# A two-layer encoder on one core: GpSimd negates weight halves between its two DMAs, and two query and key tiles change PSUM banks

## The chip, the core and the metric

The kernel runs on one core of a Trainium2 chip. The metric is device time in microseconds (us) of one execution, lower is better. The engines are TensorE (PE in the rows; PEld is its weight load), VectorE (DVE), ScalarE (ACT), GpSimd (POOL) and SyncE (SP). Each engine works through its own instructions strictly in their order, and waits at an instruction until what it needs is there. DMAs are issued by an engine's queue and land later.

## The reference, cut to what matters

Two layers; each mixes 512 tokens of 1024 channels by attention heads and a recurrent branch side by side, and then goes through a gated MLP. All of it is float32.

```python
def reference(x, g_mix, w_in, ...):
    for l in range(DEPTH):                       # DEPTH = 2
        h = rmsnorm(x, g_mix[l])
        z = h @ w_in[l]                          # 512 x 1024 by 1024 x 2560
        q, k, v, x_rec, gate = jnp.split(z, ...)  # 512 columns each
        att = neighbourhood_attention(q, k, v, rel_bias[l])
        xc = depthwise_conv(x_rec, conv_lru_w[l], conv_lru_b[l], LRU_PAD)
        rec = (rg_lru(xc, ..., reverse=False) + rg_lru(xc, ..., reverse=True)) * gelu(gate)
        mixed = concatenate([rmsnorm(att, g_att[l]), rmsnorm(rec, g_rec[l])])
        x = x + mixed @ w_out[l]
        h = rmsnorm(x, g_ffn[l])
        u_act, u_lin = jnp.split(h @ w_up[l], 2, axis=-1)
        u_act = depthwise_conv(u_act, conv_ffn_w[l], conv_ffn_b[l], (1, 1))
        x = x + (gelu(u_act) * u_lin) @ w_down[l]
    return rmsnorm(x, g_final)
```

## The kernel before

**Products in halves.** Each float32 operand is kept as two numbers: a leading half (`hi`, rounded to the format that TensorE reads) and the rest (`lo` = value - `hi`). One 128 x 128 block of weights times 512 tokens is three matmuls (`mm3`, L248 to L250): hi by hi, hi by the tokens' lo, lo by hi. So a product of a chunk of weights can start when its `hi` is there, but its third matmul (L250) needs `lo`.

**Weights.** `weight_plan` cuts all weights into chunks of eight blocks (128 x 1024 numbers, 512 KB; those of the recurrent gates have four blocks, 256 KB) in the order in which TensorE uses them. `chunk` hands out the next one and has `split_to` and `load_to` start the work on later ones. Most chunks come by SP's DMA as `raw` and are split by ScalarE and VectorE (L210, L211). Twenty chunks of the first layer, those of query, key, value, gate and the recurrent gates, are split without VectorE: GpSimd's queue issues a DMA that writes `hi` (L175), ScalarE writes `lo` = -`hi` (L200), and GpSimd's queue issues a second DMA that adds the same weights onto `lo` (L201). In the second layer these chunks come ready split, by SP. There are four buffers for `hi` and four for `lo`.

**The first layer's mixing stage.** Before it, four banks gather the recurrent input (tile `xr`) and the row sums of squares give the tokens' scale `g_mix_rb` (rows L387 to L401; GpSimd takes the power in between, L392). Then the list `MIX` gives the steps, in TensorE's order: `q`, `k`, `v`, `g` are the projections of one tile of 128 columns each (24 matmuls, an a and a b half), `t` the recurrent gates, `c` the convolution, `S` the scores of a head, `T` the transposes of its probabilities, `P` its product with the values, `u` the values turned to tokens. It runs four rounds, one for each pair of heads and each quarter of the recurrent channels; here they are called rounds one to four.

**What ScalarE and VectorE do there.** ScalarE evaluates the gates (L548 to L554), a square root for both directions (L560), the exponentials of the scores (L682) and the gelu (L636), and copies transposed tiles out of PSUM (L611 `vh`, L708 `pt`). VectorE finishes the gates (L555, L556, L562), runs two scans (L565, L568), reads the scores (L675), scales the probabilities (L684, L686), and writes the rests (`vl`, `pt`, L612 and L709). For the product `P`, GpSimd copies pieces of `vh` and `vl` into the tiles `edge` (L616).

**Order.** The program is recorded by a scheduler that places urgent work (`urgent`, and the negation with level 1) ahead of other work on each engine by its own estimate of times. The order on each engine is then fixed.

**Banks.** PSUM has eight banks of 128 x 512 numbers in four pools: `ps_mm` (three), `ps_s` (two, for the scores), `ps_pt` (two, for the transposes), `ps_o` (one).

Of the kernel before, what the change touches and what calls it, by code (L numbers as in the profile page):

```python
# [11 lines left out]
AF = mybir.ActivationFunctionType  # L12
ALU = mybir.AluOpType
# [87 lines left out]
def encoder(ctx: ExitStack, tc: tile.TileContext, x_d, w_d, cols_d, bias_d, out_d):  # L101
    nc = tc.nc
    plan = weight_plan()

    def pool(name, bufs, space=None):
        kw = {"space": space} if space is not None else {}
        return ctx.enter_context(tc.tile_pool(name=name, bufs=bufs, **kw))
# [16 lines left out]
    ps_mm = pool("ps_mm", 3, PS)  # L124
    ps_s = pool("ps_s", 2, PS)
# [3 lines left out]
    def big(pl, tag, name, dt=F32):  # L129
        return pl.tile([P, T], dt, tag=tag, name=name)  # L130

    def psum(pl, name):
        return pl.tile([P, T], F32, tag="ps", name=name)
# [6 lines left out]
    def f32(ap):  # L140
        return ap.bitcast(F32)

    def urgent(level=2):
        return tc.high_priority(offset=level * URGENT) if level else ExitStack()
# [6 lines left out]
    def pieces(i):  # L151
        return (slice(0, 1024),) if i else (slice(0, 512), slice(512, 1024))

    def width(i):
        return P * len(plan[i][2])

    def by_dma(i):

        w, _, bs = plan[i]
        return w == "gate" or w == "w_in" and bs[0][1] != 12  # L160

    def load_to(n):
        while state["load"] < min(n, len(plan)):
            i = state["load"]
            if by_dma(i):
                if i > state["use"] + 3:
                    return
                highs[i] = p_hi.tile([P, 1024], F32R, tag="hi", name=f"hi{i}")
                if i in kept:
                    lows[i] = p_lo.tile([P, 1024], F32R, tag="lo", name=f"lo{i}")  # L170
                    for n, t in enumerate((highs[i], lows[i])):
                        for h in range(width(i) // 512):
                            nc.sync.dma_start(f32(t[:, 512 * h:512 * h + 512]), kept[i][n, h])
                else:
                    nc.gpsimd.dma_start(highs[i][:, :width(i)], w_d[i][:, :width(i)])  # L175
                state["load"] += 1
                continue
            raws[i] = p_raw.tile([P, 1024], F32, tag="raw", name=f"raw{i}")
            for n, sl in enumerate(pieces(i)):
                nc.sync.dma_start(raws[i][:, sl], w_d[i][:, sl])  # L180
                if i == n == 0:
                    nc.sync.dma_start(x[0], x_d[0])
            state["load"] += 1

    def split_to(n):
        while state["split"] < min(n, len(plan)):
            i = state["split"]
            if by_dma(i) and i > state["use"] + 2:
                return
            load_to(i + 1)  # L190
            if i in kept:
                halves[i] = highs.pop(i), lows.pop(i)
                state["split"] += 1
                continue
            if i in highs:
                hi = highs.pop(i)
                lo = p_lo.tile([P, 1024], F32R, tag="lo", name=f"lo{i}")
                with urgent(1):
                    ws = slice(0, width(i))
                    nc.scalar.activation(lo[:, ws], f32(hi[:, ws]), AF.Copy, scale=-1.0)  # L200
                    nc.gpsimd.dma_start(lo[:, ws], w_d[i][:, ws], accum_op=ALU.add)  # L201
                halves[i] = (hi, lo)
                state["split"] += 1
                continue
            raw = raws.pop(i)
            hi = p_hi.tile([P, 1024], F32R, tag="hi", name=f"hi{i}")
            lo = p_lo.tile([P, 1024], F32R, tag="lo", name=f"lo{i}")
            with urgent(0):
                for sl in pieces(i):
                    nc.scalar.activation(hi[:, sl], raw[:, sl], AF.Copy)  # L210
                    nc.vector.tensor_tensor(out=lo[:, sl], in0=raw[:, sl], in1=f32(hi[:, sl]), op=ALU.subtract)  # L211
            halves[i] = (hi, lo)
            state["split"] += 1
# [22 lines left out]
    def chunk(w, l, first):  # L236
        i = state["use"]
        assert plan[i][0] == w and plan[i][1] == l and plan[i][2][0] == first, (plan[i], w, l, first)
        split_to(i + 1 + AHEAD_SPLIT)
        load_to(i + 1 + AHEAD_LOAD)  # L240
        state["use"] += 1
        return halves.pop(i)
# [26 lines left out]
    def column_parts(ps, w, l, m, rhs, step):  # L269
        c = chunk(w, l, (0, m))  # L270
        for k in range(8):
            mm3(ps, blk(c, k), rhs[k], k == 0, k == 7)
            if k % step == step - 1:
                yield
# [130 lines left out]
    def by_group(ap):  # L405
        return ap.rearrange("p (r g c) -> p g r c", r=ROWS, c=8)

    def in_group(ap):
        return ap.rearrange("p g (r c) -> p g r c", r=ROWS)
# [82 lines left out]
    def layer(l, xn):  # L492
# [79 lines left out]
        qk = {}  # L572

        def query_tile(i):
            ps = psum(ps_mm, f"qps{l}{i}")
            yield from column_parts(ps, "w_in", l, i, xg, 4)
            with urgent():
                for n in range(2):
                    rows = slice(64 * n, 64 * n + 64)
                    nc.vector.tensor_tensor(out=in_group(q_pair[rows, :, n]), in0=by_group(ps)[rows],  # L580
                                            in1=by_group(rb)[rows], op=ALU.mult)

        def key_tile(i):
            ps = psum(ps_mm, f"kps{l}{i}")
            yield from column_parts(ps, "w_in", l, 4 + i, xg, 4)
            qk[4 + i] = big(p_h, "h", f"k{l}{i}")
            with urgent():
                nc.vector.scalar_tensor_tensor(out=qk[4 + i], in0=ps, scalar=0.125, in1=rb, op0=ALU.mult, op1=ALU.mult)
# [123 lines left out]
        def products(h, t1, t2):  # L712
# [22 lines left out]
            if h % 2:  # L735
# [6 lines left out]
                att_stats.add(at)  # L742

        tiles = {"q": query_tile, "k": key_tile, "v": value_tile, "g": gate_tile}
        going, probs, turned = {}, {}, {}
        ops, ocs, bias = {}, {}, {}
# [87 lines left out]
        for hf in range(2):  # L834
# [39 lines left out]
            for m in range(4, 6 if last else 8):  # L874
                ps = psum(ps_s if m % 2 else ps_pt, f"dn{l}{hf}{m}")
# [79 lines left out]
```

## Time and profile before

| | us |
|---|---|
| runs shown: median of three (lowest, highest) | 1227.52 (1226.66, 2701.48) |
| the profiled execution | 1226.75 |
| its span, first to last instruction | 1224.0 |
| TensorE busy | 1198.3 (98%) |
| VectorE busy | 736.7 (60%) |
| ScalarE busy | 503.7 (41%) |
| GpSimd busy | 123.7 (10%) |

The profile has one row for each instruction or group of them, with the time that the engine stood idle before it and what ended the idle time ("<- ACT lo L200": ScalarE's instruction of line 200 that writes `lo`). The chain of waits goes back from a last instruction to what released it, and so on. TensorE is busy in 98% of the span; what it stands idle before the MLP lies almost wholly in the first layer's mixing stage, from 22 us to 150 us.

### The profile page before, as it was taken

To read this page: it belongs to the slowest core of one execution; us is meant where nothing else is said; L and a number is where in the kernel's file an instruction comes from. 1 tells how busy PE (TensorE), PEld (TensorE's weight loads), DVE (VectorE), ACT (ScalarE), POOL (GpSimd) and SP (SyncE) were. 2 spreads that over 40 slices of the span, in tenths; PEclk is the share of its full clock that TensorE was granted. 3 is DMA by queue.
4 is the path that set the end of the run, shared out by engine and by line. 5 is a ranking of instruction groups with operands and counts; after the bars stand their busy time and mean duration, and the time that the engine had idled before them with its cause. 6 is when DMAs were issued, how large, how long until landed. Compare 5 with 4: busy or idle time off the path is not lost.

```text
span 1224.0 us, 14611 instructions
## 1 busy us (share of the span) xinstructions
PE 1198.3 (98%) x5566; PEld 999.0 (82%) x5566; DVE 736.7 (60%) x1217; ACT 503.7 (41%) x741; POOL 123.7 (10%) x206
## 2 busy tenths in 40 slices
PE   9888999999999999999999999999999999999997
PEld 7777788888888888888888888888888888888886
DVE  6476684877653376662736777677556255555454
ACT  5566783544332144332416667443322212323220
POOL 3222210022220022210000100100000000000000
PEclk9999999999999999999999999999999999999999
DMA  8656632366663366653245443142232332322322
GB/s 270 142 133 124 140 104 70 103 206 213 229 217 99 102 216 224 215 171 103 92 132 191 141 148 104 38 136 90 100 104 88 101 103 86 104 93 96 103 69 69
DMA packets 53942, 161.29 MB, mean 132 GB/s; under 512 B 6768, under 2 KB 9968, under 8 KB 53872
## 3 DMA queue, kind: packets, MB, share of 16 engines
q1 hardware_dynamic: 39328, 113.17, 28.3%
q0 software_dynamic: 14400, 47.20, 14.1%
q8 instruction: 43, 0.70, 0.2%
q14 instruction: 27, 0.22, 0.1%
q10 hardware_dynamic: 144, 0.00, 0.0%
HBM read 139.37 MB, written 20.97 MB: 131 GB/s over the span
## 4 chain that ended last, share of the span: by engine, by line
PE 90%; DVE 4%; issue 3%; DMA 1%; POOL 1%; ACT 1%; POOLq 0%; DVEq 0%; ACTq 0%
PE dn L248 7%; PE dn L250 7%; PE dn L249 7%; PE pa L248 7%; PE pl L248 7%; PE pa L249 7%; PE pl L249 7%; PE pl L250 7%; PE pa L250 7%; PE out L250 2%; PE out L248 2%; PE out L249 2%; DMA hi<-in_w 1%; PE up L248 1%; PE up L250 1%
## 5 line engine op out<-in xcount | busy, mean ns | idle before, releaser
L210 ACT ACTIVATE hi<-raw 128x1024 fp32r<-128x1024 f32 (+1 forms) x169 | 178.3, 1055 | 388.3 <-PE dn L249 160.5
L211 DVE TENSOR_TENSOR lo<-raw,hi 128x1024 fp32r<-128x1024 f32 (+1 forms) x169 | 205.3, 1215 | 133.5 <-ACT hi L210 132.7
L818 DVE TENSOR_TENSOR ua<-pa,g_ffn_rb 128x512 f32<-128x512 f32 x44 | 30.4, 692 | 113.7 <-PE pa L250 113.7
L826 ACT ACTIVATE uc<-uc,cols 128x512 f32<-128x512 f32 x48 | 34.8, 724 | 115.9 <-DVE uc L824 115.9
L827 DVE TENSOR_TENSOR uc<-pl,uc 128x512 f32<-128x512 f32 x44 | 30.3, 689 | 44.6 <-PE pl L250 43.8
L466 POOL TENSOR_TENSOR fin_r<-fin_ms,expo 128x2 f32<-128x2 f32 x2 | 1.4, 697 | 377.7 <-DVE fin_ms L464 377.7
L795 DVE TENSOR_TENSOR dns<-dn,g_ffn_rb 128x512 f32<-128x512 f32 x30 | 20.5, 689 | 29.4 <-PE dn L250 29.4
L233 POOL DMA_DIRECT2D kept<-lhi x36 | 19.5, 543 | 177.8 <-ACT lhi L227 174.5
L824 DVE SCALAR_TENSOR_TENSOR uc<-ua,cols,uc 128x511 f32<-128x511 f32 x48 | 36.0, 750 | 1.5
L822 DVE SCALAR_TENSOR_TENSOR uc<-ua,cols,uc 128x511 f32<-128x511 f32 x48 | 35.7, 744 | 0.1
L200 ACT ACTIVATE lo<-hi 128x1024 fp32r<-128x1024 f32 (+1 forms) x20 | 19.4, 972 | 32.7 <-DMA hi<-in_w 24.6
L228 DVE TENSOR_TENSOR llo<-lraw,lhi 128x512 fp32r<-128x512 f32 x36 | 24.7, 687 | 10.7 <-ACT lhi L227 10.7
L682 ACT ACTIVATE prob<-prob,mx 128x192 f32<-128x192 f32 (+1 forms) x64 | 27.5, 430 | 1.1 <-DVE mx L680 0.9
L248 PE MATMUL out<-atth,hi 128*128 128x512 f32 x64 | 25.7, 402 | 0.0
L249 PE MATMUL out<-attl,hi 128*128 128x512 f32 x64 | 25.2, 394 | 0.0
L201 POOL DMA_DIRECT2D lo<-in_w x20 | 17.5, 877 | 75.8 <-ACT lo L200 75.8
L250 PE MATMUL out<-atth,lo 128*128 128x512 f32 x64 | 25.2, 393 | 0.0
L616 POOL CAST edge<-vh 64x384 fp32r<-64x384 f32 x16 | 10.1, 629 | 144.3 <-ACT vh L611 143.8
L233 POOL DMA_DIRECT2D kept<-llo x36 | 19.5, 543 | 48.9 <-DVE llo L228 46.3
L821 DVE TENSOR_SCALAR uc<-ua,cols 128x512 f32<-128x512 f32 x48 | 23.4, 487 | 1.6
L667 PE MATMUL s<-k,q_pair 128*128 128x192 f32 (+1 forms) x128 | 22.0, 314 | 2.4 <-DVE mx L675 2.4
L556 DVE SCALAR_TENSOR_TENSOR ti<-ti,xc 128x512 f32<-128x512 f32 x16 | 11.0, 689 | 21.9 <-ACT ti L548 21.9
(934 smaller groups left out, 3687.2 us busy)
## 6 DMA issues: line engine op xcount, KB each, us to landing
raw<-in_w SPq DMA_DIRECT2D x167, 512.0 KB, 3.5
lraw<-in_w POOLq DMA_DIRECT2D x36, 256.0 KB, 4.2
kept<-lhi POOLq DMA_DIRECT2D x36, 256.0 KB, 2.5
kept<-llo POOLq DMA_DIRECT2D x36, 256.0 KB, 3.0
hi<-kept SPq DMA_DIRECT2D x36, 256.0 KB, 2.8
lo<-kept SPq DMA_DIRECT2D x36, 256.0 KB, 4.0
hi<-in_w POOLq DMA_DIRECT2D x16, 512.0 KB, 5.4
lo<-in_w POOLq DMA_DIRECT2D x16, 512.0 KB, 5.6
```

The source lines that it names most:

```text
L210: nc.scalar.activation(hi[:, sl], raw[:, sl], AF.Copy)
L211: nc.vector.tensor_tensor(out=lo[:, sl], in0=raw[:, sl], in1=f32(hi[:, sl]), op=ALU.subtract)
L233: nc.gpsimd.dma_start(d, f32(parts[h][n]))
L248: nc.tensor.matmul(ps, a[0], b[0], start=start, stop=False)
L249: nc.tensor.matmul(ps, a[0], b[1], start=False, stop=False)
L250: nc.tensor.matmul(ps, a[1], b[0], start=False, stop=stop)
L682: nc.scalar.activation(pr[b], pr[b], AF.Exp, bias=mx[:, b % 4:b % 4 + 1], accum_out=sm[:, b % 4:b % 4 + 1])
L818: nc.vector.tensor_tensor(out=ua, in0=pa, in1=rbf[0], op=ALU.mult)
L822: nc.vector.scalar_tensor_tensor(out=c[:, 1:], in0=ua[:, :T - 1], scalar=w[0], in1=c[:, 1:], op0=ALU.mult, op1=ALU.add)
L824: nc.vector.scalar_tensor_tensor(out=c[:, :T - 1], in0=ua[:, 1:], scalar=w[2], in1=c[:, :T - 1], op0=ALU.mult, op1=ALU.add)
L826: nc.scalar.activation(c, c, AF.Gelu_apprx_tanh, bias=col("conv_ffn_b", j, l))
L827: nc.vector.tensor_tensor(out=c, in0=pl_, in1=c, op=ALU.mult)
```

## The change

The negation (L200) is done by GpSimd and no longer by ScalarE. And the first query tile and the first key tile of a layer are gathered in the two banks of the scores' pool (`ps_s`) and not in two of `ps_mm`.

```diff
@@ in split_to @@
                 with urgent(1):
                     ws = slice(0, width(i))
-                    nc.scalar.activation(lo[:, ws], f32(hi[:, ws]), AF.Copy, scale=-1.0)
+                    nc.gpsimd.tensor_scalar(out=lo[:, ws], in0=f32(hi[:, ws]), scalar1=-1.0, scalar2=None, op0=ALU.mult)
                     nc.gpsimd.dma_start(lo[:, ws], w_d[i][:, ws], accum_op=ALU.add)
@@ in query_tile @@
-            ps = psum(ps_mm, f"qps{l}{i}")
+            ps = psum(ps_mm if i else ps_s, f"qps{l}{i}")
@@ in key_tile @@
-            ps = psum(ps_mm, f"kps{l}{i}")
+            ps = psum(ps_mm if i else ps_s, f"kps{l}{i}")
```

The order of instructions changes on three engines. TensorE's and SP's stay the same. On GpSimd, at the start of the mixing stage (`hi_233` and `lo_267` are the first query's chunk, `hi_270` and `lo_340` the first key's, `hi_343` and `lo_417` that of the first recurrent gates, `hi_420` and `lo_458` the first value's; a minus is before, a plus is the change):

```order
 L175 DMA hi_233<-in_w 128x1024
 L175 DMA hi_270<-in_w 128x1024
+L200 TENSOR_SCALAR lo_267<-hi_233 128x1024
 L201 DMA lo_267<-in_w 128x1024
+L200 TENSOR_SCALAR lo_340<-hi_270 128x1024
+L392 TENSOR_TENSOR g_mix_r<-g_mix_ms,expo 128x4
 L175 DMA hi_343<-in_w 128x512
 L201 DMA lo_340<-in_w 128x1024
-L392 TENSOR_TENSOR g_mix_r<-g_mix_ms,expo 128x4
+L200 TENSOR_SCALAR lo_417<-hi_343 128x512
 L201 DMA lo_417<-in_w 128x512
 L175 DMA hi_420<-in_w 128x1024
```

The negations now stand in GpSimd's queue, one ahead of each second DMA, and the power L392 has moved ahead of the DMAs of `hi_343` and `lo_340`.

On ScalarE, in round two (`a_849` and `a_852` belong to the recurrent gates, `w_784` is what the square root is taken of, `prob_159` and `prob_160` are two heads' probabilities):

```order
 L376 ACTIVATE att_acc<-att_732 128x512
 L551 ACTIVATE a_849<-w_784,spn 128x512
-L200 ACTIVATE lo_946<-hi_867 128x1024
+L376 ACTIVATE rec_acc<-fb_533 128x512
 L552 ACTIVATE w_784<-w_784,sp 128x512
+L554 ACTIVATE a_852<-a_849 128x512
+L560 ACT_TABLE_LOAD
+L560 ACTIVATE w_784<-w_784 128x1024
+L682 ACT_TABLE_LOAD
 L682 ACTIVATE prob_159,sm_888<-prob_159,mx_887 128x128
 L682 ACTIVATE prob_159,sm_888<-prob_159,mx_887 128x192 x3
```

The square root L560 stood behind these four exponentials and two negations, and stands ahead of the exponentials now.

On VectorE, in round two (`ti` and `w` go into the two scans, `sm_888` and `prob_159` are the sums and probabilities of the round's first head):

```order
+L562 TENSOR_TENSOR ti_785<-ti_785,w_784 128x512
 L680 TENSOR_SCALAR mx_923<-mx_923 128x4
-L562 TENSOR_TENSOR ti_785<-ti_785,w_784 128x512
 L562 TENSOR_TENSOR ti_838<-ti_838,w_784 128x512
-L632 TENSOR_TENSOR z_997<-gate_945,g_mix_rb 128x512
 L565 SCALAR_TENSOR_TENSOR fb_858<-a_796,ti_785 128x512
 L568 SCALAR_TENSOR_TENSOR w_784<-a_849,ti_838 128x512
+L684 RECIPROCAL sm_888<-sm_888 128x4
+L570 TENSOR_TENSOR fb_858<-fb_858,w_784 128x512
+L686 TENSOR_SCALAR prob_159<-prob_159,sm_888 128x128
+L686 TENSOR_SCALAR prob_159<-prob_159,sm_888 128x192 x3
```

The scaling of the first head's probabilities, which stood ahead of the scans, stands behind them now.

## Rows read from the trace of the kernel before

**Rows 1.** Busy time by stretch: stretch, length, engines' busy us, granted clock, DMA, GB/s.
```profile
22.00:76.00 54.00, 45.41 (x211) 36.10 (x210) 32.31 (x88) 26.24 (x46) 14.99 (x22) 0.99 0.67 148
76.00:114.00 38.00, 34.71 (x170) 29.35 (x169) 23.57 (x59) 26.52 (x46) 9.93 (x14) 0.95 0.56 124
114.00:150.00 36.00, 33.54 (x172) 28.50 (x171) 24.87 (x61) 26.52 (x47) 10.11 (x14) 0.98 0.63 137
```

**Rows 2.** TensorE in order of time: start, us, line, tiles [idle before <- what ended it].
```profile
30.83 0.50 PE L248 MATMUL qps<-xg_g_mix_0h,hi 128*128 128x512 f32 x1 [1.47 <-DVE xrs L515]
...
72.49 0.39 PE L248 MATMUL o<-pt,vh 128*128 128x256 f32 x1 [2.81 <-ACT vh L611]
...
74.35 0.33 PE L250 MATMUL o<-pt,edge 128*128 128x128 f32 x1 [0.47 <-POOL edge L616]
...
101.13 0.60 PE L699 MATMUL ptw<-ident,prob 128*128 128x128 f32 x4
...
110.84 0.39 PE L249 MATMUL o<-pt,vh 128*128 128x256 f32 x1 [2.87 <-ACT lo L200]
...
147.07 0.39 PE L249 MATMUL o<-pt,vh 128*128 128x256 f32 x1 [1.95 <-ACT lo L200]
```

**Rows 3.** Chain of waits that ends at 75 us, from 22 us: start, us, what.
```profile
22.49 6.37 DMA hi<-in_w
...
28.93 0.64 ACT lo L200
...
29.87 0.93 POOL lo L201
...
64.78 5.57 DMA hi<-in_w
...
70.37 1.06 ACT lo L200
...
71.72 0.86 POOL lo L201
72.58 0.52 POOL edge L616
```

**Rows 4.** GpSimd in order of time, two instructions at the stage's start.
```profile
22.49 0.54 POOL L175 DMA_DIRECT2D hi<-in_w  x1
...
24.56 1.32 POOL L392 TENSOR_TENSOR g_mix_r<-g_mix_ms,expo 128x4 f32<-128x4 f32 x1
```

**Rows 5.** ScalarE in order of time, in round two.
```profile
100.43 0.64 ACT L200 ACTIVATE lo<-hi 128x512 fp32r<-128x512 f32 x1 [4.66 <-issue]
...
102.38 1.06 ACT L560 ACTIVATE w<-w 128x1024 f32<-128x1024 f32 x1
```

**Rows 6.** VectorE in order of time, in rounds two and three.
```profile
103.47 1.29 DVE L562 TENSOR_TENSOR ti<-ti,w 128x512 f32<-128x512 f32 x2 [5.94 <-ACT w L560]
...
108.38 1.21 DVE L686 TENSOR_SCALAR prob<-prob,sm 128x192 f32<-128x192 f32 x4
...
111.16 0.54 DVE L709 TENSOR_TENSOR pt<-pte,pt 128x384 fp32r<-128x384 f32 x1
...
139.70 1.29 DVE L562 TENSOR_TENSOR ti<-ti,w 128x512 f32<-128x512 f32 x2 [4.00 <-ACT w L560]
```

**Rows 7.** Groups by line and shape: count, busy us, mean ns, idle before them.
```profile
L200 ACT ACTIVATE lo<-hi 128x1024 fp32r<-128x1024 f32 x16 | 16.9, 1057 | 19.4 <-DMA hi<-in_w 19.2
...
L313 POOL MEMSET prob<- 128x1024 f32 x2 | 1.9, 948 | 0.0
```

**Rows 8.** Copies of GpSimd into tile edge: ns min/median/max, first and last start.
```profile
L616 POOL CAST edge<-vl x16: 502/507/1367, 73.7 to 770.0; 64x384 fp32r<-64x384 f32 x16
```

**Rows 9.** DMA issues, 10 to 170 us: count, KB, median us to landing.
```profile
lo<-in_w POOLq DMA_DIRECT2D x4, 256.0 KB, 4.0
```

**Rows 10.** Busy time by stretch, with the granted clock, after TensorE's pause in round two.
```profile
112.00:114.00 2.00, 2.00 (x12) 2.00 (x12) 1.96 (x4) 0.00 (x0) 1.02 (x2) 0.56 0.49 98
114.00:116.00 2.00, 2.00 (x9) 1.76 (x8) 1.92 (x5) 1.07 (x2) 0.00 (x0) 0.59 1.05 246
```

## The prediction

> **What bounds the kernel now.** I read the busy times by stretch first, to see where TensorE is not busy. In round one (22 to 76 us) it stands idle 54.00 - 45.41 = 8.6 us, in round two (to 114 us) 38.00 - 34.71 = 3.3 us, in round three (to 150 us) 36.00 - 33.54 = 2.5 us [rows 1]. That is 14.4 us of 1224, so no cure of these waits can bring 2%.
>
> Then TensorE's own rows, for what ended the idle time. In round one it waits 1.47 us for VectorE to empty the recurrent input's banks before the first query tile, and 2.81 us for ScalarE's `vh` before the first product P; in rounds two and three 2.87 and 1.95 us, each before a P [rows 2]. Each name leads back to ScalarE, and the change frees ScalarE. Whether it helps depends on what was late behind ScalarE, and there the rounds differ.
>
> The chain of waits shows round one. It does not run through TensorE at all between 22.5 and 74 us: it is GpSimd's queue. A DMA of `hi` is issued at 22.49 us and takes 6.37; ScalarE negates at 28.93; GpSimd issues the second DMA at 29.87 and behind it the next `hi`, and so on, until a `hi` issued at 64.78 is negated at 70.37, its second DMA is issued at 71.72, and only then does GpSimd come to the `edge` copies at 72.58 [rows 3], for which TensorE waits, last at 74.35 [rows 2]. So TensorE's waits in round one are slack along a longer chain. Take one away, and TensorE comes earlier to P and waits there longer.
>
> Round two is another case. ScalarE stands idle 4.66 us, with its square root behind the negation that waits for a `hi`; the root runs at 102.38 [rows 5], and VectorE stands idle 5.94 us for it; its last `pt` then ends at 111.16 + 0.54 = 111.70 [rows 6], while TensorE came to P at 110.84 - 2.87 = 107.97 [rows 2]. Round three has the same picture: VectorE is idle 4.00 us for the root [rows 6], TensorE 1.95 for P [rows 2]. Here ScalarE's place in the queue is on the path.
>
> **The change, part by part.** The sum is made against the profiled execution's own 1226.75 us (span 1224.0, the rest lies around it); the median of the runs shown is 0.8 us above it.
>
> *The banks.* The first query tile no longer waits for the recurrent input's banks (1.47 us [rows 2]). ScalarE without its negations would copy the tokens' scale earlier and so free these banks anyway. Both only make TensorE earlier in round one, so I cost the edit at nothing. What hides it is the chain [rows 3]; were that cover gone, it and the freed ScalarE could return up to the 8.6 us.
>
> *The start of the chain.* The power L392 now stands ahead of the DMA of `hi_343`, with which the chain begins. It started at 24.56 and took 1.32 us [rows 4]; its input comes from TensorE's sums, which the change leaves in place. So this DMA goes out at about 25.9 and not at 22.49, 3.4 us late. But it took 6.37 us then, beside two others of twice its size; the 256 KB DMAs of the other kind took 4.0 [rows 9]. Its landing moves by between 3.4 - 2.4 = 1.0 and 3.4. I take 4.5 us for it, since one DMA still follows right behind: 3.4 - 1.9 = +1.5.
>
> *The negations on the chain.* From there to the `edge` copies six of the twenty lie on the chain: two of 512 columns and four of 1024. Before, one of 1024 cost 71.72 - 70.35 = 1.37 us from landing (64.78 + 5.57) to the second DMA, one of 512 cost 29.87 - 28.86 = 1.0 [rows 3]; ScalarE's own part is 1.057 [rows 7]. The trace has no such instruction on GpSimd. From below: a fill of 1024 columns takes 0.95 [rows 7], and it reads nothing. From above: the copies into `edge`, 384 columns with the same types, take 0.507 in the median and 1.367 at worst [rows 8], in proportion 1.35 and 3.65 for 1024. I take 1.4, near the median, and 0.15 more to the DMA (between nothing and the 0.3 us that ScalarE's word to GpSimd took: 71.72 - 70.37 - 1.06 [rows 3]): 1.55, so +0.18 for each of the four. By the same scale 512 columns cost 0.85, so -0.15 for each of the two. Together +0.4. With 0.95 and no distance it is 4 x -0.42 + 2 x -0.52 = -2.7; with 3.65 and 0.3 it is 4 x 2.58 + 2 x 1.13 = +12.6.
>
> The Trainium skill, GPSIMD Engine Reference, section "Engine selection", calls GpSimd's one-input elementwise work roughly line-rate, and its "Specifications" give 1.2 GHz; an estimate from that page is 1024 / 1.2 GHz = 0.85 us. By it the forecast below would be about 1219 us. The nearest rows, 0.507 us for 384 columns, are 0.19 us slower than that rate, and no row of this kernel has the negation itself.
>
> *Round one in sum:* +1.5 + 0.4 = about +2. TensorE's idle time gathers before P instead of lying in five places, so I expect one wait of 7 to 8 us there. The granted clock fell to half after the pause of round two [rows 10]; I assume as much slow time after the pause of round one as before, and keep 1.7 us either way for the range.
>
> *Round two.* ScalarE no longer waits, and by its new order the root stands ahead of the exponentials, so VectorE can go on where it stood idle, at 103.47 - 5.94 = 97.53 [rows 6]; 1.2 earlier than that, since the scaling of the first head's probabilities (1.21 [rows 6]) has moved behind the scans: 96.3. The end of `pt` came 111.70 - 103.47 = 8.2 us after that start; with the scaling 9.4: 105.7, ahead of TensorE's 107.97. So the 3.3 us of idle time go. What is late next is that scaling: it ends, by the rows from L562 to the other head's scaling (103.47 to 109.59, less 0.6 for `z`, which has moved behind), 5.5 us after 96.3, at 101.8, and TensorE wants the transposes at 101.13 [rows 2]. That is a new wait of 0 to 1.5 us; I take 0.5. With the pause, the slow clock goes: 0.56 and 0.59 granted over 4 us [rows 10], which cost 2 x 0.44 + 2 x 0.41 = 1.7 us. Round two: -3.3 + 0.5 - 1.7 = -4.5.
>
> *Round three.* VectorE gains 4.00 us on a wait of 2.5 us of TensorE's [rows 1, 6]: -2.5. No slow clock to win: the mean over the round is 0.98 with the tail of round two's in it [rows 1].
>
> *The other negations.* Two stand ahead of the power, at the very start; twelve lie in rounds two to four, where GpSimd is busy 10 of 38 us [rows 1] and the DMAs wait for TensorE to free buffers: nothing. `edge` copies queue behind one negation of 512 columns there, some 3 us ahead of P.
>
> The sum: +2 - 4.5 - 2.5 = -5.0, so 1226.75 - 5.0 = 1221.75, about **1222 us**.
>
> **The rivals.**
>
> *Slower: GpSimd's negation is long.* VectorE and GpSimd hold each other up where both read SBUF: the copies into `edge` range from 0.502 to 1.367 us for one shape [rows 8]. Each us on the 1024-column negation costs round one 4 + 2 x 0.5 = 5 us. The gain of 7.0 is eaten once +2 + 5 x (N - 1.4) = 7, at N = 2.4 us. At the worst copy's 3.65 us it is +1.5 + 12.6 - 7.0 = +7: 1234 us. For it: VectorE is busy 60% of round one. Against it: the median copy is at the minimum. The Trainium skill, SBUF — State Buffer, section "Who interferes with whom", has this as a lock: a VectorE instruction with two SBUF inputs and a GpSimd instruction that reads SBUF block each other for the whole instruction. By that rule the cost is at most one VectorE instruction for each negation.
>
> *VectorE takes ScalarE's place.* In rounds two and three the scaling of the first head now stands behind the scans. If it comes 3 us later than I work out, the transposes wait what P waited: 1226.75 + 2 = 1229 us. Against it: 5.94 us of idle time ahead of it [rows 6].
>
> *Round one gains too.* If the `edge` copies were not what P waits for, all of TensorE's idle time could go: 1226.75 - 14.4 - 1.7 = about 1211 us. Against it: the last links of the chain [rows 3], which the new order leaves as they are, negation, DMA, then the copies.
>
> **How the numbers follow.** Forecast, 0.66: 1222, with a range of its own of 1218 to 1225 (the first DMA's bounds, the negation from 0.95 to 1.7 us, the clock). Slower by a long negation, 0.13: 1226 to 1234. VectorE in ScalarE's place, 0.14: 1226 to 1230. Round one gains, 0.07: 1211 to 1217. The range leaves out the last and the upper part of the second: 1217 to 1230. No case reaches 2%, about what a measurement of this kernel can tell from no change (1203 and 1252), so faster 0.02, same 0.96, slower 0.02, the ends for a price beyond these bounds.
>
> **What the profile after would show.** Right: the first `hi_343` DMA at about 26 us; GpSimd's L200 at 1.2 to 1.7 us; the first `edge` copy at 74 to 75 us and TensorE idle 7 to 8 us before the first P; no wait before P in rounds two and three, and VectorE's waits for the root gone; a wait below 1.5 us at the transposes of round two. Wrong: L200 above 2.4 us on GpSimd; an `edge` copy before 71 us; waits of 2 us and more at the transposes; weights that TensorE waits for in rounds two to four; a second stretch of slow clock in round one.

## The result, and the profile after

The changed kernel takes 1248.0 us (median of four, 1245.9 to 1248.6) against 1227.1: a ratio of 1.017, interval 1.015 to 1.019. That is 21 us slower, where 5 us faster was forecast. The profiled execution took 1245.85 us, with a span of 1244.1 (before 1224.0). One of the four runs of the kernel before took 2701.5 us and is not in the ratio.

The first thing to read is the moved instruction itself. Groups by line and shape of the changed kernel (count, busy us, mean ns, idle time before them); on ScalarE it was 1057 ns [rows 7]:

```profile
L200 POOL TENSOR_SCALAR lo<-hi 128x1024 fp32r<-128x1024 f32 x16 | 47.1, 2941 | 46.9 <-DMA hi<-in_w 31.4 <-issue 15.5
L200 POOL TENSOR_SCALAR lo<-hi 128x512 fp32r<-128x512 f32 x4 | 6.4, 1612 | 16.4 <-issue 9.7 <-PE pte L703 5.1 <-DMA hi<-in_w 1.7
```

2.94 us, where 1.4 was taken, and from its end to the second DMA 0.30 us. GpSimd in order of time shows what that does to the chain of round one, which began in [rows 3] and ended there with the `edge` copies at 72.58 us:

```profile
21.84 2.85 POOL L200 TENSOR_SCALAR lo<-hi 128x1024 fp32r<-128x1024 f32 x1
26.13 1.04 POOL L392 TENSOR_TENSOR g_mix_r<-g_mix_ms,expo 128x4 f32<-128x4 f32 x1 [1.45 <-DVE g_mix_ms L389]
27.15 0.62 POOL L175 DMA_DIRECT2D hi<-in_w  x1
...
38.67 2.77 POOL L200 TENSOR_SCALAR lo<-hi 128x1024 fp32r<-128x1024 f32 x1 [5.01 <-DMA hi<-in_w]
41.74 0.91 POOL L201 DMA_DIRECT2D lo<-in_w  x1 [0.30 <-POOL lo L200]
42.34 0.89 POOL L175 DMA_DIRECT2D hi<-in_w  x1
48.58 2.77 POOL L200 TENSOR_SCALAR lo<-hi 128x1024 fp32r<-128x1024 f32 x1 [5.35 <-issue]
...
81.31 2.77 POOL L200 TENSOR_SCALAR lo<-hi 128x1024 fp32r<-128x1024 f32 x1 [4.75 <-issue]
84.37 0.91 POOL L201 DMA_DIRECT2D lo<-in_w  x1 [0.30 <-POOL lo L200]
84.98 1.40 POOL L616 CAST edge<-vh 64x384 fp32r<-64x384 f32 x2
```

One link, from a negation to the next, is 48.58 - 38.67 = 9.9 us; before, ScalarE negated the same two chunks 8.1 us apart:

```profile
36.17 1.06 ACT L200 ACTIVATE lo<-hi 128x1024 fp32r<-128x1024 f32 x1 [6.12 <-DMA hi<-in_w]
44.27 1.06 ACT L200 ACTIVATE lo<-hi 128x1024 fp32r<-128x1024 f32 x1 [3.58 <-DMA hi<-in_w]
```

The `edge` copies start at 84.98, 12.4 us later than before. TensorE in order of time, its waits (answering to [rows 2]):

```profile
47.17 0.63 PE L250 MATMUL vps<-xg_g_mix_0h,lo 128*128 128x512 f32 x1 [2.48 <-DMA lo<-in_w]
67.82 0.79 PE L250 MATMUL qps<-xg_g_mix_0h,lo 128*128 128x512 f32 x1 [3.85 <-DMA lo<-in_w]
85.86 0.47 PE L248 MATMUL o<-pt,edge 128*128 128x128 f32 x1 [10.81 <-POOL edge L616]
...
143.60 0.50 PE L250 MATMUL gate<-xg_g_mix_0h,lo 128*128 128x512 f32 x1 [2.16 <-DMA lo<-in_w]
```

All waits of TensorE's matmuls in the mixing stage are now for GpSimd: 1.20 us for the power at 27.23, the others for `edge` or for a `lo` whose second DMA was issued late. None is for VectorE. The wait before P in round two (2.87 us [rows 2]) is gone, as forecast, but new ones of the other kind stand in rounds three and four.

The end of each round's first product P (the last matmul of the tile `o`, from TensorE's rows) gives the loss round by round. The kernels below the first two are experiments of the next section; "price" is GpSimd's mean time for 1024 columns:

| kernel | price, us | round one | two | three | four |
|---|---|---|---|---|---|
| before | (ScalarE) | 75.93 | 113.43 | 149.34 | 179.27 |
| changed | 2.94 | 88.86 | 122.75 | 165.15 | 199.32 |
| copy in all chunks | 1.15 | 76.75 | 110.36 | 142.99 | 173.12 |
| multiplication in the first nine only | 2.88, 1.23 | 88.88 | 122.33 | 154.71 | 184.64 |
| multiplication in the last eleven only | 1.19, 2.96 | 75.56 | 109.98 | 153.42 | 188.35 |
| half of the columns multiplied | 2.30 | 83.23 | 116.06 | 154.12 | 186.08 |

Changed against before: +12.9 us at the end of P in round one, +9.3 in round two, +15.8 in round three, +20.1 in round four, and +20.1 in the span. So round one lost 12.9, round two won 3.6, rounds three and four lost 6.5 and 4.2.

### The profile page after: what moved, and what is told of

Its sections match the earlier page's. It is cut to its first block, busy times and chain, and to the rows that moved or that the text cites. A ratio compares the mean times of both kernels' runs of the same rounds, so it can differ in the third digit from the quotient of the medians.

```text
span 1244.1 us, 14573 instructions
## 1 busy us (share of the span) xinstructions
PE 1203.6 (97%) x5566; PEld 1003.6 (81%) x5566; DVE 750.9 (60%) x1217; ACT 486.4 (39%) x721; POOL 176.5 (14%) x226
## 4 chain that ended last, share of the span: by engine, by line
PE 82%; DVE 2%; DMA 1%; issue 1%; POOL 1%; ACT 0%; POOLq 0%; DVEq 0%
PE dn L249 7%; PE dn L248 7%; PE dn L250 7%; PE pl L249 6%; PE pa L249 6%; PE pl L248 6%; PE pa L250 6%; PE pa L248 6%; PE pl L250 6%; PE out L250 2%; PE out L248 2%; PE out L249 2%; PE up L248 1%; PE up L249 1%; PE up L250 1%
## 5 line engine op out<-in xcount | busy, mean ns | idle before, releaser
L200 POOL TENSOR_SCALAR lo<-hi 128x1024 fp32r<-128x1024 f32 (+1 forms) x20 | 53.5, 2675 | 63.3 <-DMA hi<-in_w 33.0
L708 ACT ACTIVATE pt<-ptw 128x512 fp32r<-128x512 f32 x16 | 9.5, 596 | 56.7 <-PE ptw L699 56.7
L228 DVE TENSOR_TENSOR llo<-lraw,lhi 128x512 fp32r<-128x512 f32 x36 | 24.7, 688 | 10.7 <-ACT lhi L227 10.7
L686 DVE TENSOR_SCALAR prob<-prob,sm 128x192 f32<-128x192 f32 (+1 forms) x64 | 26.0, 469 | 0.2
L250 PE MATMUL out<-atth,lo 128*128 128x512 f32 x64 | 25.2, 394 | 0.0
L249 PE MATMUL out<-attl,hi 128*128 128x512 f32 x64 | 25.2, 394 | 0.0
L733 DVE COPY att<-o 64x256 f32<-64x256 f32 x32 | 13.5, 420 | 18.2 <-PE o L250 17.9
```

Of the source, the lines that this page charges most:

```text
L200: nc.gpsimd.tensor_scalar(out=lo[:, ws], in0=f32(hi[:, ws]), scalar1=-1.0, scalar2=None, op0=ALU.mult)
L249: nc.tensor.matmul(ps, a[0], b[1], start=False, stop=False)
L250: nc.tensor.matmul(ps, a[1], b[0], start=False, stop=stop)
```

## The experiments

The theory (A): the whole loss is the length of GpSimd's instruction, in the one queue that issues both DMAs of a chunk. The rivals: the new banks (B); the queue itself, that is, the power ahead of the first DMA and DMAs that now stand behind GpSimd's own work (C); the `edge` copies' place at the end of the chain.

**The banks alone.** ScalarE negates as before.

```diff
-                    nc.gpsimd.tensor_scalar(out=lo[:, ws], in0=f32(hi[:, ws]), scalar1=-1.0, scalar2=None, op0=ALU.mult)
+                    nc.scalar.activation(lo[:, ws], f32(hi[:, ws]), AF.Copy, scale=-1.0)
```

> The kernel before with the change of banks alone; ScalarE negates as before. No instruction changes its place on any engine. Theory A (the loss is the length of GpSimd's negation, 2.94 us for 1024 columns where ScalarE took 1.06, in the one queue that brings the weights): 1226 to 1228 us, the 1.47 us wait before the first query tile gone and as much added before the first P. Rival B (the scores' banks, held by a projection, delay the scores of the first heads): 1235 us or more, with new waits at the scores of round one.

Measured: 1227.0 us, ratio 1.000 (0.999 to 1.002). The 1.47 us before the first query tile are gone; TensorE waits elsewhere in round one instead, for instance 3.10 us at the scores (before 2.39). They were expected before the first P; the wait there was 2.41, before 2.81. P of round one ends at 76.04, before at 75.93. The banks are worth nothing here, as the prediction had it.

**The negation alone**, with the old banks (the two lines of the banks undone).

> GpSimd negates, the old banks; the order on every engine is that of the changed kernel. Theory A: 1246 to 1250 us, the first edge copy again near 85 us. Rival B: at least 8 us faster than the changed kernel, 1240 or less.

Measured: 1246.8 us, ratio 1.016 (1.014 to 1.019). The loss belongs to the negation; rival B falls. The first `edge` copy came at 87.66 us, not near 85, in a profiled execution that was the slowest of the four (1250.1).

**A copy in the negation's place.** Same queue, same order on every engine.

```diff
-                    nc.gpsimd.tensor_scalar(out=lo[:, ws], in0=f32(hi[:, ws]), scalar1=-1.0, scalar2=None, op0=ALU.mult)
+                    nc.gpsimd.tensor_copy(out=lo[:, ws], in_=f32(hi[:, ws]))
```

> The changed kernel with a plain copy of the leading half in the negation's place on GpSimd, same tiles, same queue order on all engines; the sign is left out. Theory A, first form (it is the multiplication by a number that is long; a copy goes like the edge copies, 1.35 us for 1024 columns): 1220 to 1226 us, the sum of the prediction. Theory A, second form (any GpSimd instruction on this tile is long, by its 128 partitions or the change of type): the copy takes 2.5 us or more and the kernel stays at 1244 to 1250. Rival C (not the length but the queue: the power ahead of the first DMA, and DMAs that now stand behind work of GpSimd): 1235 or more although the copy takes 1.4 us.

Measured: 1220.7 us, ratio 0.995 (0.993 to 0.997). By the group of its line, by shape, the copy takes 1.15 us:

```profile
L200 POOL CAST lo<-hi 128x1024 fp32r<-128x1024 f32 x16 | 18.4, 1147 | 48.1 <-DMA hi<-in_w 29.4 <-issue 15.8 <-PE qps L250 2.9
```

This is nearly the kernel that the prediction described (1.15 us where it took 1.4), and it takes nearly the time that the prediction gave. GpSimd and TensorE in order of time:

```profile
26.03 0.61 POOL L175 DMA_DIRECT2D hi<-in_w  x1
...
70.99 1.04 POOL L200 CAST lo<-hi 128x1024 fp32r<-128x1024 f32 x1 [4.99 <-issue]
72.33 0.87 POOL L201 DMA_DIRECT2D lo<-in_w  x1 [0.30 <-POOL lo L200]
72.88 1.39 POOL L616 CAST edge<-vh 64x384 fp32r<-64x384 f32 x2
```

```profile
73.76 0.48 PE L248 MATMUL o<-pt,edge 128*128 128x128 f32 x1 [8.31 <-POOL edge L616]
```

The first `hi` DMA at 26.03 (forecast "about 26"), one wait of 8.3 us before P in round one (forecast 7 to 8), none before P in rounds two and three. So the queue's new order costs little by itself (P of round one ends 0.8 us later than before), and rival C falls. The first form of theory A holds: it is the multiplication by a number that is long, not the tile, its 128 partitions or the output's type.

**The negation on VectorE.**

```diff
-                    nc.gpsimd.tensor_scalar(out=lo[:, ws], in0=f32(hi[:, ws]), scalar1=-1.0, scalar2=None, op0=ALU.mult)
+                    nc.vector.tensor_scalar(out=lo[:, ws], in0=f32(hi[:, ws]), scalar1=-1.0, scalar2=None, op0=ALU.mult)
```

> The changed kernel with the negation on VectorE, same instruction otherwise. By the rows of VectorE's TENSOR_SCALAR on 512 columns (0.487 us) it takes 0.97 us for 1024. Theory A: 1220 to 1232 us, depending on what stands ahead of it in VectorE's queue; the lower end if VectorE comes to it at once. Rival C (ScalarE's queue was the right place because it is free; any other engine's queue costs the same as GpSimd's): 1240 or more.

Measured: 1230.0 us, ratio 1.003 (1.001 to 1.004). The group of its line shows 0.70 us, a quarter of GpSimd's:

```profile
L200 DVE TENSOR_SCALAR lo<-hi 128x1024 fp32r<-128x1024 f32 x16 | 11.1, 695 | 18.8 <-DMA hi<-in_w 18.1 <-PE s L667 0.6
```

It is no gain, because VectorE now stands at negations whose DMAs have not landed (18.1 us in all), and what is queued behind it is late: TensorE waits 4.66 us at the scores of round one, and at the transposes of rounds two and three. TensorE's rows:

```profile
105.42 1.02 PE L699 MATMUL ptw<-ident,prob 128*128 128x128 f32 x4 [2.14 <-DVE prob L686]
142.83 0.93 PE L699 MATMUL ptw<-ident,prob 128*128 128x128 f32 x4 [3.40 <-DVE prob L686]
```

These are the waits of the prediction's second rival, here with VectorE at fault for another reason.

**Where the multiplication costs.** Two kernels with the order of the changed one, one line each (NEG and COPY stand for the two lines of the copying kernel's diff, `tensor_scalar` and `tensor_copy`; `i` counts all chunks, and the first of the twenty has 4):

```diff
+                    NEG if i < 13 else COPY
```

```diff
+                    COPY if i < 13 else NEG
```

> The changed kernel; GpSimd multiplies only in the first nine chunks (those up to the first edge copies) and copies in the eleven later ones, with the sign left out there. Same order on every engine. Against the kernel that copies everywhere (1220.7 us): if the chain of round one takes each added time in full, 4 x (2.94 - 1.15) + 2 x (1.61 - 0.74) = 8.9 us, and 1.1 for the first DMA, which the longer negation of the key's chunk delays: 10 us, and 1 to 3 of slow clock after the longer pause, so 1231 to 1234. Rival (the loss is made in the later rounds): below 1225.

> The reverse: copies in the first nine chunks (sign left out), the multiplication in the eleven later ones. If the later rounds cover it, as the prediction said of them: 1220 to 1223 us. If GpSimd's queue binds there too once the negation is long (in the changed kernel TensorE's work of rounds three and four came 6.5 and 5.5 us later against round two): 1230 to 1236, with waits for lo in front of the gate and query projections.

Measured: 1231.4 us (ratio 1.004, 1.003 to 1.006) and 1235.2 us (1.006, 1.004 to 1.009). Against the copying kernel that is +10.7 and +14.5, in sum 25.2 of the 27.3 between it and the changed kernel. The later rounds, which the prediction costed at nothing, cost at least about as much as round one (the two intervals overlap). TensorE's rows in round three, with the last eleven multiplied:

```profile
131.48 0.50 PE L250 MATMUL gate<-xg_g_mix_0h,lo 128*128 128x512 f32 x1 [2.48 <-DMA lo<-in_w]
141.69 0.50 PE L250 MATMUL qps<-xg_g_mix_0h,lo 128*128 128x512 f32 x1 [3.17 <-DMA lo<-in_w]
149.93 0.33 PE L248 MATMUL o<-pt,edge 128*128 128x128 f32 x1 [2.61 <-POOL edge L616]
```

And GpSimd's rows there: the negations of the value chunks of rounds three and four, 42.8 us apart, where TensorE gets through a round in 154.71 - 122.33 = 32.4 us when it waits for nothing (fourth row of the table).

```profile
112.15 2.77 POOL L200 TENSOR_SCALAR lo<-hi 128x1024 fp32r<-128x1024 f32 x1 [2.60 <-DMA hi<-in_w]
...
122.32 3.06 POOL L200 TENSOR_SCALAR lo<-hi 128x1024 fp32r<-128x1024 f32 x1 [5.62 <-issue]
...
154.97 2.76 POOL L200 TENSOR_SCALAR lo<-hi 128x1024 fp32r<-128x1024 f32 x1 [2.90 <-PE pte L703]
```

A turn that is longer than TensorE's round costs nothing as long as the queue is ahead. In the copying kernel the same two chunks were copied at 109.13 and 145.36 us, 36.2 us apart; TensorE's round from P to P took 142.99 - 110.36 = 32.6, and no matmul of rounds two to four waited more than 0.15 us for a weight. With the multiplication the lead is gone in round two, and in round three TensorE takes 153.42 - 109.98 = 43.4 us, nearly the queue's turn.

**Half of the columns multiplied**, the other half copied: a price between the two.

```diff
-                    nc.gpsimd.tensor_scalar(out=lo[:, ws], in0=f32(hi[:, ws]), scalar1=-1.0, scalar2=None, op0=ALU.mult)
+                    hs, gs = slice(0, width(i) // 2), slice(width(i) // 2, width(i))
+                    nc.gpsimd.tensor_scalar(out=lo[:, hs], in0=f32(hi[:, hs]), scalar1=-1.0, scalar2=None, op0=ALU.mult)
+                    nc.gpsimd.tensor_copy(out=lo[:, gs], in_=f32(hi[:, gs]))
```

> The changed kernel with half of the columns of each chunk multiplied and the other half copied by GpSimd (the sign left out in that half), two instructions one behind the other, same order of all else. By the rows of earlier runs 1.49 us and 0.6 to 0.75 us, so 2.1 to 2.3 us for a chunk, halfway between copy (1.15) and multiplication (2.94). If round one takes each added time in full and the later rounds cover this much (a threshold above 2.2 us): 5 us above the copying kernel's 1220.7, 1225 to 1227. If the later rounds have no cover beyond the copy: half of the whole loss, 1232 to 1236.

Measured: 1234.1 us, ratio 1.007 (1.004 to 1.009). The two took 1.71 and 0.69 us in the mean, 2.30 from the start of the first to the end of the second. 13.4 us for 1.15 us of price is 12 us for each us; from copy to multiplication it is 27.3 for 1.79, 15 for each us. In round one alone (table) it is 6.5 / 1.15 = 5.6 and 12.1 / 1.79 = 6.8, near the prediction's 5. The later rounds had less cover than the theory with a threshold above 2.2 us asked for.

**The edge copies on ScalarE**, the negation left on GpSimd.

```diff
-                        nc.gpsimd.tensor_copy(e[rows, dst], src[rows, cs])
+                        nc.scalar.activation(e[rows, dst], f32(src[rows, cs]), AF.Copy)
```

> The changed kernel with ScalarE making the edge copies, so that no consumer but the weights stands behind the chain in GpSimd's queue; the negations stay on GpSimd. If it is the edge copies' place at the end of the chain that costs (10.8 us of wait before P in round one): 1234 to 1238 us. If the weights behind the same chain are as late and TensorE only waits for them instead, at the next key projection (its lo landed at 90.0 us, when TensorE would come to it near 80): 1243 to 1249.

Measured: 1244.3 us, ratio 1.015 (1.013 to 1.017). P of round one now ends at 76.68 with no wait at all, 12.2 us earlier than in the changed kernel, and most of it is given back: the time is 3.7 us lower, and the two intervals overlap. TensorE's rows in the next round:

```profile
90.80 0.50 PE L250 MATMUL vps<-xg_g_mix_0h,lo 128*128 128x512 f32 x1 [3.30 <-DMA lo<-in_w]
...
111.61 0.49 PE L250 MATMUL qps<-xg_g_mix_0h,lo 128*128 128x512 f32 x1 [2.28 <-DMA lo<-in_w]
```

The weights come through the same chain. The `edge` copies were the place of the wait, not its cause.

**What ScalarE's place in the queue is worth.** ScalarE negates, with the new banks, but with the lowest urgency.

```diff
-                with urgent(1):
+                with urgent(0):
```

> ScalarE negates as before, with the new banks, but the negation is given the lowest urgency, so that in rounds two and three the square root and the first head's exponentials stand ahead of the negations that wait for a DMA. If ScalarE's place in the queue was worth 3.3 + 2.5 us in rounds two and three, as the prediction has it: 1219 to 1224 us. Rival (the stall moves to whatever stands behind the negation now): 1226 to 1230.

Measured: 1220.0 us, ratio 0.995 (0.994 to 0.997). P of rounds two and three starts without the 2.87 and 1.95 us of [rows 2] (in round three it waits 0.68 us, for ScalarE's gelu); its ends, 73.97, 107.31 and 140.23 us, come 2.0, 6.1 and 9.1 us earlier than before. Round four of the profiled execution gives a part back (P ends at 176.11, 3.2 us earlier than before), with waits of 1.15 us for ScalarE's gates and 1.47 for VectorE's scaling. So the stalls of ScalarE's queue were real, and a number in the program's order removes them; the rival, that the stall moves on, holds for round four alone.

**VectorE with the lowest urgency, without and with ScalarE's edge copies.** `nc.vector.tensor_scalar` and `urgent(0)`; the second with the edit of the `edge` copies above.

> VectorE negates with the lowest urgency, the edge copies stay on GpSimd: what of the earlier 1217.8 us (VectorE, lowest urgency, edge copies on ScalarE) belongs to the edge copies. If the edge copies behind the chain delay P in round one: 2 to 5 us slower than that run, 1220 to 1223, with a wait before P. If not: 1217 to 1219.

> VectorE negates (0.70 us for 1024 columns in an earlier run) with the lowest urgency, and ScalarE makes the edge copies, which then no longer stand behind the chain in GpSimd's queue. If the edge copies behind the last link are what P waits for in round one: P starts 2 to 4 us earlier there, and with ScalarE free of the negations 1214 to 1222 us. Rival (VectorE's queue becomes the bound, as in the earlier run with VectorE, where the transposes waited 2 to 3 us for the scaling): 1226 to 1232.

Measured: 1220.0 us (0.995, 0.993 to 0.996) and 1217.8 us (0.993, 0.992 to 0.995). The lower urgency turns the 1230 us of VectorE's first run into 1220. What the `edge` copies add is not settled: the intervals overlap. P of round one ends at 76.07 and 74.64 us, and no wait above 0.31 stands before it in either, so the expected wait did not show. In the second run TensorE still waits at the scores of round one, for VectorE's negation:

```profile
56.66 2.71 PE L667 MATMUL s<-k,q_pair 128*128 128x192 f32 x8 [4.89 <-DVE mx L675]
```

**Both engines.** The first seven chunks by ScalarE, which has time in round one, the thirteen later ones by VectorE, all with the lowest urgency, `edge` copies by ScalarE.

```diff
+                    ACT if i < 11 else VEC
```

(ACT is ScalarE's line of the first experiment, VEC VectorE's line of the fourth.)

> ScalarE negates the first seven chunks and VectorE the thirteen later ones, all with the lowest urgency, and ScalarE makes the edge copies. In the run with VectorE alone TensorE waited 4.9 us at the scores of round one, for VectorE, which stood at a negation whose DMA had not landed. If that wait goes: 1212 to 1216 us. If round one is bound by the weights' chain in any case: 1216 to 1219, the wait at another place.

Measured: 1215.0 us, ratio 0.991 (0.989 to 0.993), the lowest median of all kernels here; its interval overlaps that of VectorE alone (0.992 to 0.995). That wait has shrunk:

```profile
52.31 1.46 PE L667 MATMUL s<-k,q_pair 128*128 128x192 f32 x8 [0.83 <-DVE mx L675]
```

In round three, where VectorE negates, TensorE waits 2.75 us at the scores (125.44): VectorE stood 5.38 us at a negation whose DMA had not landed.

## Why the prediction was wrong

**The step that failed first: the price of the negation.** The prediction bounded it by a fill (0.95 us) and the copies into `edge` (1.35 in proportion, 3.65 at worst), took "1.4, near the median", and gave the long negation a chance of 0.13. It measured 2.94. The copy of the same tile measured 1.15, so the scaling by columns was sound to 0.25 us; what failed was to take rows of one operation for another. The bounds held it, the choice between them didn't, and the upper one held it by luck: it came from the one `edge` copy that took 1.367 us where the median took 0.507, and the negation is long each time. Contention, the rival's reason for a long negation, is a small part: nine of the sixteen took 2.77 to 2.85 us, the other seven 3.10 to 3.29.

**The second: "The other negations ... nothing".** It rested on GpSimd being busy 10 of 38 us [rows 1] and on DMAs that wait for TensorE to free buffers. Busy time is the wrong measure of a queue that works in order and stands most of its time at DMAs: what counts is how long a round takes through it, 42.8 us against TensorE's 32.4, and how far ahead of TensorE it is. In the kernel before, its `hi` DMAs waited 6.8 us for TensorE in round two:

```profile
84.73 0.57 POOL L175 DMA_DIRECT2D hi<-in_w  x1 [3.92 <-PE kps L250]
87.49 0.56 POOL L175 DMA_DIRECT2D hi<-in_w  x1 [2.19 <-PE gp L250]
...
94.19 0.57 POOL L175 DMA_DIRECT2D hi<-in_w  x1 [0.68 <-PE vps L250]
```

That was the cover, against five negations in a round that became 4 x (2.94 - 1.06) + (1.61 - 0.64) = 8.5 us longer. And the cover lasts only as long as TensorE is late itself: with copies, where TensorE no longer waits before the P of round two, these waits are 7.1 us in round two, but 0.6 in round three, where they were 6.3 before. So the gain that the prediction counted on uses up the cover that it counted on. In the changed kernel 4.15 us of it are left in round two and none in round three. So even the prediction's own rival, with the price measured, would have given 1226.75 + 2 + 5 x (2.94 - 1.4) - 7.0 = 1229, and the time is 1248: the slope from copy to multiplication was 15 us for each us (12 up to 2.30 us, 22 above), not 5.

**The third, small: the start of the chain and its count.** The power's input is not TensorE's sums alone, which the change leaves in place: VectorE's mean square (L389) stands between them, and it came at 25.89 us instead of 24.26, for a reason given in the last section. So the first `hi` DMA went out at 27.15, not 25.9. It took 3.0 us, not 4.5, and landed at about 30.2 against 28.85 before: the +1.5 that was taken came out by luck, of two errors. With the copy it went out at 26.03, took 3.0 us too and landed at about 29.0: some +0.1. The count of six negations on the chain held for a short price only. Two of the chunks are fetched by one pair of DMAs; before, they were negated 2.04 us apart, as they landed, and one of the two negations cost the chain nothing. At 3.1 us each both lie on the chain, 4.12 us apart, which is 2.1 of the 12.9 us of round one. The prediction had put one of them among the twelve of rounds two to four. Before (first two lines) and changed:

```profile
53.06 1.06 ACT L200 ACTIVATE lo<-hi 128x1024 fp32r<-128x1024 f32 x1 [2.38 <-DMA hi<-in_w]
55.10 1.06 ACT L200 ACTIVATE lo<-hi 128x1024 fp32r<-128x1024 f32 x1 [0.47 <-DMA hi<-in_w]
...
58.97 3.17 POOL L200 TENSOR_SCALAR lo<-hi 128x1024 fp32r<-128x1024 f32 x1 [5.29 <-DMA hi<-in_w]
63.09 3.11 POOL L200 TENSOR_SCALAR lo<-hi 128x1024 fp32r<-128x1024 f32 x1
```

**The fourth: the clock.** Slow clock followed the longer wait before P in round one, and came in rounds three and four too, for which the prediction had no slow clock. Busy times by stretch of the changed kernel, columns as in [rows 1], from the end of that wait on, and over rounds three and four:

```profile
86.00:90.00 4.00, 3.56 (x16) 3.37 (x17) 0.84 (x2) 0.25 (x1) 1.91 (x4) 0.50 0.95 204
88.90:92.00 3.10, 3.10 (x12) 2.75 (x11) 2.46 (x5) 1.09 (x2) 0.46 (x1) 0.54 0.57 184
92.00:96.00 4.00, 4.00 (x19) 3.25 (x19) 0.94 (x2) 2.00 (x3) 3.70 (x2) 1.00 0.00 0
...
150.00:186.00 36.00, 29.33 (x135) 23.83 (x133) 20.65 (x46) 20.04 (x32) 16.91 (x15) 0.91 0.63 133
186.00:222.00 36.00, 34.35 (x176) 28.93 (x177) 20.87 (x40) 14.84 (x30) 4.95 (x6) 0.95 0.11 35
```

0.50 is the lower of the two levels, 1.2 GHz; the full 2.4 came back at about 92 us. TensorE had stood idle 10.81 us ahead of it. From 86 to 92 us this cost some 2.9 us; before, the four us behind P of round one (75 to 79) had 0.61, which is 1.6. So the assumption of "as much slow time after the pause of round one as before" was 1.3 us short, inside the 1.7 that the prediction kept for it. Behind the waits for weights that end at 154.25 (3.63 us) and 187.65 (3.13 us) the clock was at 0.50 again, from 154.2 to 160 and from 187.6 to 190.5 us, and 0.64 in the mean from 187.6 to 192: some 2.9 and 1.6 us more. Before, it was 1.00 from 116 to 200 us, and the slow clock behind round two's pause, 1.7 us, is gone. On the path, then, slow clock cost some 7.4 us, before 3.3: 4 of the 21 us are clock, each stretch of it behind one of these waits.

**Right:** round one is bound by GpSimd's chain (+5.6 and +6.8 us of P for each us of price, where 5 was worked out). The banks are worth nothing. ScalarE's stalls in rounds two and three are on the path: with the copy, round two won 3.9 us (forecast 4.5) and round three 3.3 (forecast 2.5); no wait before P in either, and at the transposes no more than 0.31. The forecast sum was -5.0 us; the copying kernel, with 1.15 us for the forecast 1.4, measured 0.995 of before, which is -6 us. The sum comes so near in part by luck: its terms are off by 1.2 us in round one (+0.8 for +2) and by 0.6 and 0.8 in rounds two and three, in part against each other. VectorE in ScalarE's place did not become the bound.

Of the signs that the prediction listed as wrong, three came: L200 above 2.4 us, weights that TensorE waits for in rounds two to four, and a second stretch of slow clock in round one (0.72 in the mean from 46 to 52 us and again from 66 to 72, ahead of the one from 78 on).

## What to carry to other kernels

An instruction is moved to an engine with the price of that operation on that engine; a copy of the same tile there says little about a multiplication. An engine whose queue issues DMAs and also works between them is judged by the time of one turn through that queue and by its lead, not by its busy share, and once the lead is used up, whatever is put into that queue is paid in every turn. And where the trouble is that one engine stands at a transfer ahead of work that is ready, look first at the order: a lower urgency for the waiting instruction gave here what the move to another engine was meant to give.

## What the runs showed of the hardware

**GpSimd's price depends on the operation.** At their shortest, a copy of 512 and 1024 columns took 0.62 and 1.04 us, so 0.8 ns for a column more; the multiplication by a number 1.49 and 2.77, 2.5 ns for a column more, with some 0.2 us for the start of each. VectorE did the same multiplication in 0.70 us, ScalarE in 1.06. The Trainium skill, GPSIMD Engine Reference, section "Engine selection", has one-input work as roughly line-rate: the trace agrees for the copy, and not for the multiplication, which is three times that.

**VectorE pays for GpSimd's negations.** One line, `L686` (a scaling by a number for each partition), by its durations in the kernel changed, and with the copy (min, median and max ns):

```profile
L686 DVE TENSOR_SCALAR prob<-prob,sm x64: 260/314/3751, 59.5 to 787.6; 128x192 f32<-128x192 f32 x48, 128x128 f32<-128x128 f32 x16
```

```profile
L686 DVE TENSOR_SCALAR prob<-prob,sm x64: 259/314/1335, 54.9 to 761.3; 128x192 f32<-128x192 f32 x48, 128x128 f32<-128x128 f32 x16
```

The longest one (from 62.56 us, 3.75 long) ended with a GpSimd negation (63.09 to 66.20). The same shows at the start, where it reaches the chain. VectorE in order of time, beside the negation that GpSimd ran from 21.84 to 24.69:

```profile
21.85 1.13 DVE L338 TENSOR_SCALAR sp_s<-sp_e 128x16 f32<-128x16 f32 x1 [0.30 <-ACT sp_e L337]
23.02 0.25 DVE L339 RECIPROCAL sp_q<-sp_s 128x16 f32<-128x16 f32 x1
23.30 0.17 DVE L340 TENSOR_TENSOR sp_s<-sp_e,sp_q 128x16 f32<-128x16 f32 x1
23.51 0.17 DVE L341 TENSOR_TENSOR sp_s<-sp_s 128x16 f32<-128x16 f32 x1
23.72 1.00 DVE L342 TENSOR_SCALAR sp_q<-sp_s 128x16 f32<-128x16 f32 x1
```

In the kernel before, L338 and L342 took 0.17 us each. Some 1.8 us of VectorE's time went there, the mean square for the power (L389) came late, the power with it, and behind the power the first `hi` DMA of the chain. The Trainium skill, SBUF — State Buffer, section "Who interferes with whom", says that a scaling of this kind can hold or be held by GpSimd for a whole instruction; the trace agrees for the longest L686 and for L342, which end with the negation, and not for L338, which took 1.13 us and ended 1.7 us ahead of it. The same section has a VectorE instruction with two SBUF inputs held too; here L340, with two inputs of 16 columns, took 0.17 us beside the negation, as before, and was not held.
